# Three sub-layer boundaries of a two-layer decoder trunk, worked on 512 tokens at once instead of in two halves

## The chip, the core and the metric

The kernel runs on one core of a Trainium2 chip. That core has a matrix engine (TensorE, "PE" in the profile), an elementwise engine (VectorE, "DVE"), an activation engine (ScalarE, "ACT"), a general engine (GpSimd, "POOL") and DMA queues, most of them issued by SyncE ("SP"). Each engine executes its own instructions in the order in which the program wrote them, and waits for others by semaphores. On-chip operands lie in SBUF; matmul results lie in PSUM. The metric is the device time of one execution in microseconds (us), as the median of several runs.

## The reference

Two layers, one sequence of 512 tokens, 1024 features, FFN width 2816. Layer 0 mixes tokens by stick-breaking attention, layer 1 by sparse attention that an indexer selects. Each mixer, and each gated MLP behind it, gets a normed, scaled and shifted input, and its result is gated onto x:

```python
for i in range(DEPTH):
    mod = cond @ ada_w[i] + ada_b[i]
    sh1, sc1, g1, sh2, sc2, g2 = split(mod, 6)
    h = rms_norm(x, norm_mix[i]) * (1.0 + sc1) + sh1
    x = x + g1 * mixer_i(h)          # h @ w_in, attention, @ w_out
    h = rms_norm(x, norm_ffn[i]) * (1.0 + sc2) + sh2
    x = x + g2 * conv_ffn(h)         # u = h @ w_up; width-3 causal conv; silu(gate) * val; @ w_down

def rms_norm(x, g):                  # y = x / sqrt(mean(x*x) + 1e-6) * g
def dsa_attention(h, w_in, ...):     # proj = h @ w_in: 16 queries of 128, a latent of 128,
                                     # 8 indexer queries of 64, one indexer key of 64, 8 weights
```

So with s = gain * (1 + scale), a projection behind a norm is W^T (x * s * r) + W^T shift, where r is one number per token.

## The kernel before

Activations lie with features on the partitions and tokens along the row: x is eight tiles `x0` to `x7` of 128 features x 512 tokens. Every number that PE multiplies is split into a high part in a reduced format (fp32r) and the remainder, and each product is three matmuls (`mm3`, L250 to L252): high by high, low weight by high, high weight by low. A weight chunk of 128x1024 (512 KB) is loaded by DMA into one of six buffers of the pool `raws`, ACT copies its high part (`split_hi`, L210, tile `whi`), and DVE, or in the layer-1 attention sometimes POOL, subtracts for the low part (`split_lo`, L218, tile `wlo`). There are four `whi` and four `wlo` buffers. `order` lists the chunks in the order of their use; `fetch` loads ahead along it, and `chunk(key)` hands out a finished pair.

Nothing reorders the program: on each engine the instructions stand in the order in which the Python code issues them.

A **boundary** is the stretch from the last output projection of one sub-layer to the first projections of the next. There are three: 1 from layer 0's attention to its MLP, 2 from that MLP to layer 1's attention, 3 from that attention to layer 1's MLP (the start of the kernel and the last projection, `final_proj`, are written apart). In each, `last` names the four chunks of the output projection (eight result tiles `pt_l` of 128 features, each a sum over four 128-deep steps of three matmuls) and `first` the first four chunks of the next sub-layer: two pairs of gate and value columns of the MLP's up projection, or, in boundary 2, `kw` (indexer key and weights) and three query chunks. Their results are `pt_first`, eight steps of three matmuls each.

Before, a boundary goes through the tokens in two halves of 256 columns:

- half 0: per tile, the output projection, the update of x (`add_to_x`, L372 and DVE), ACT's square (`sqt`, five buffers), and the sum of the squares over tiles on DVE (`sqa`, L295);
- half 1 likewise, and among it the norm of half 0: the sum over features by a matmul with `ones_mean` (`pt_norm`, L300), ACT's reciprocal root as a seed (tile `ln`), one Newton step in three DVE instructions (`norm_newton`, L334 to L336), then per tile `u = r * sfac * x` on DVE (L343), the high part `hhi` with the shift on ACT, and the low part `hlo` on DVE (L352). The squares of half 1 are summed by PE itself in quarters (`quarter_squares`, tile `pt_part`, L307);
- the first two chunks on half 0, with the norm of half 1 among them, then the other two on half 0;
- `second_half`: the four chunks on half 1, each with what its `finish` does to the result. In the MLPs that is the evacuation `evac_up` with the width-3 convolution (tile `y`: one ACT and two DVE instructions, L998 to L1000), and after each second tile `mix` (L1017 a product, then the split into `acthi` and `actlo`, L234 and L235). In boundary 2 it copies the indexer keys `kd`, `kl` and queries; the indexer's scores `z` follow.

Matmuls in the boundaries therefore have 256 columns, elsewhere 512. `ada_dot` (L259) computes the modulation vectors `mod` on DVE from streamed chunks; it runs all through layer 0.

Of the kernel before, what the change touches and what calls it, by code (L numbers as in the profile page):

```python
# [18 lines left out]
D = 1024  # L19
# [40 lines left out]
def chunk_order():  # L60
    keys = []
    for l in range(DEPTH):
        for g in range(6):
            keys += [("ada", l, g, k) for k in range(KT)]
    for p in range(PAIRS):
        keys += [("q", p), ("k", p)]
    for g in range(4):
        keys += [("v", g, h) for h in range(2)]
    for nm in ("o", "do"):
        for g in range(2):  # L70
            keys += [(nm, g, m) for m in range(4)]
# [8 lines left out]
    keys += [("uv",)]  # L80
    return {k: i for i, k in enumerate(keys)}
# [38 lines left out]
def kernel_body(ctx, tc, xT, wst, cst, smalls, crow, ccol, relb, onehot, outT):  # L120
# [30 lines left out]
    sfac = cpool.tile([P, KT], F32, name="sfac")  # L151

# [132 lines left out]
    def square(f, hf):  # L285
        t = npool.tile([P, H2], F32, name="sqt", bufs=5)
        act.activation(t, x[f][:, halves[hf]], AF.Square)
        return t

    def square_add(f, t):  # L290
        if f == 0:
            a = sqs["acc"] = npool.tile([P, H2], F32, name="sqa")
# [4 lines left out]
    def sum_squares(t, start, stop):  # L297
        if start:
            sqs["pt"] = ptile([P, H2], "pt_norm", "z")
        pe.matmul(sqs["pt"], lhsT=ones_mean, rhs=t, start=start, stop=stop)  # L300

    def quarter_squares(ts, first):

        if first:
            sqs["parts"] = ptile([P, H2], "pt_part", "z")
        for i, t in enumerate(ts):
            pe.matmul(sqs["parts"][32 * i:32 * i + 32], lhsT=ones_mean[:, :32], rhs=t, start=first, stop=not first)  # L307

    def quarters_out():
        t = sqs["sum"] = npool.tile([P, H2], F32, name="sqt", bufs=5)  # L310
        act.activation(t, sqs["parts"], AF.Copy, scale=D / 32)
# [14 lines left out]
    def norm_seed(hf):  # L326
        ln = rstd[hf] = npool.tile([P, H2], F32, name="ln", bufs=2)
        act.activation(ln, sqs["pt"], AF.Abs_reciprocal_sqrt, bias=eps_c)
        rstd[hf, "ms"] = sqs["pt"]

    def norm_newton(hf):
        ln, ms = rstd[hf], rstd[hf, "ms"]
        t = npool.tile([P, H2], F32, name="nt")
        dve.tensor_mul(t, ln, ln)  # L334
        dve.scalar_tensor_tensor(t, ms, EPS, t, op0=OP.add, op1=OP.mult)
        dve.scalar_tensor_tensor(ln, t, 3.0, ln, op0=OP.subtract, op1=OP.mult)  # L336
# [3 lines left out]
    def norm_u(hf, f):  # L340
        c = halves[hf]
        u = us[hf, f] = npool.tile([P, H2], F32, name="u", bufs=4)
        dve.scalar_tensor_tensor(u, rstd[hf], sfac[:, f:f + 1], x[f][:, c], op0=OP.mult, op1=OP.mult)  # L343

    def norm_hi(l, sh, hf, f):
        act.activation(hcur["h"][f][0][:, halves[hf]], us[hf, f], AF.Identity,
                       bias=mod[l][:, sh * KT + f:sh * KT + f + 1])

    def norm_lo(l, sh, hf, f):
        c = halves[hf]  # L350
        hi, lo = hcur["h"][f]
        dve.scalar_tensor_tensor(lo[:, c], us.pop((hf, f)), mod[l][:, sh * KT + f:sh * KT + f + 1],  # L352
                                 hi[:, c].bitcast(F32), op0=OP.add, op1=OP.subtract)

    def norm_ops(l, sh, hf):

        for f in range(KT + 2):
            if f < KT:
                norm_u(hf, f)
                norm_hi(l, sh, hf, f)  # L360
            if f >= 2:
                norm_lo(l, sh, hf, f - 2)
            yield
# [25 lines left out]
    def boundary(last, O, l, gate, nxt, first):  # L389
# [3 lines left out]
        unsplit = lambda: pos["i"] <= order.index(last[3])  # L393
# [3 lines left out]
        fetch(pos["i"] + 1)  # L397

        begun = {}

        def out_steps(hf, m, ks):
            c = halves[hf]
            whi, wlo = cks[m // 2]
            if m not in begun:
                begun[m] = ptile([P, H2], "pt_l", "tr" if hf or m % 2 == 0 else "z")
            for k in ks:
                w = k * 256 + (m % 2) * P
                mm3(begun[m], whi[:, w:w + P], wlo[:, w:w + P], O[k][0][:, c], O[k][1][:, c], k == 0, k == 3)

        def out_tile(hf, m):  # L410

            if hf or m > 1:
                out_steps(hf, m, range(4))
            elif m == 0:
                for ks in (range(3), range(3, 4)):
                    for i in range(2):
                        out_steps(hf, i, ks)
            add_to_x(l, gate, m, begun.pop(m), halves[hf])
            return square(m, hf)

        prev = None
        for m in range(KT):
            t = out_tile(0, m)
            if prev is not None:
                square_add(m - 1, prev)
            prev = t
            if m in (0, 2) and unsplit():
                split_hi()
            if m in (1, 3):
                split_lo()  # L430
                if m == 3:
                    while unsplit():
                        split_hi()
                        split_lo()
# [4 lines left out]
        ops0 = norm_ops(nl, sh, 0)  # L439
        pend = []  # L440
        for m in range(KT):
            if m == 1:
                sum_squares(sqs["acc"], True, False)
                sum_squares(prev, False, True)
                norm_seed(0)
            if m == 5:
                quarter_squares(pend[:4], True)
            pend.append(out_tile(1, m))
            if m == 1:
                norm_newton(0)  # L450
            if m in (2, 4):
                split_hi()
            if m in (3, 5):
                split_lo()
            for _ in range((0, 0, 1, 1, 2, 1, 2, 2)[m]):
                next(ops0, None)
        for _ in ops0:
            pass
# [50 lines left out]
    def stick_layer(l):  # L509
        with ExitStack() as st:  # L510
# [445 lines left out]
            for i in range(HN):  # L956
# [16 lines left out]
                if i % 2:  # L973
# [6 lines left out]
            first = boundary([("o", 1, m) for m in range(4)], [O[4 + k] for k in range(4)], l, 2,  # L980
                             (l, S_NF, 3, 4), up_first(l))
# [5 lines left out]
    def ffn_layer(l, first, man):  # L987
        with ExitStack() as st:
# [43 lines left out]

            ys = []

            def finish(i, pt):
                ys.append(evac_up(i // 2, i % 2, pt))
                if i == 0:
                    warm(AF.Silu)
                if i % 2:
                    mix(i // 2, *ys[-2:])  # L1040

            second_half(first, finish)
# [13 lines left out]
            if l < DEPTH - 1:  # L1056
                return boundary(last, O, l, 5, (l + 1, S_NM, 0, 1),
                                [("kw",), ("qi", 0), ("qi", 1), ("qi", 2)]), man
# [3 lines left out]
    def dsa_layer(l, first, man):  # L1062
        with ExitStack() as st:
# [92 lines left out]
            with ExitStack() as si:  # L1156
# [18 lines left out]
                def finish(i, pt):  # L1175
                    if i:
                        if i < 3:
                            qi_evac(i - 1, pt)
                        return
                    act.activation(kd[:64], pt[:64], AF.Copy)  # L1180
                    act.activation(kd[64:], pt[:64], AF.Copy)
                    dve.tensor_sub(kl[:64], pt[:64], kd[:64].bitcast(F32))
                    dve.tensor_sub(kl[64:], pt[:64], kd[64:].bitcast(F32))
                    act.activation(kw, pt, AF.Copy)
# [5 lines left out]
                second_half(first, finish, (0, 2))  # L1190
# [54 lines left out]
                for h in range(IDX_HEADS):  # L1245
# [12 lines left out]
                    if h == 0:  # L1258
                        qi_evac(2, first[1][3])
# [442 lines left out]
```

## Time and profile before

| | us |
|---|---|
| time, median of 3 runs | 1281.17 (1280.67 to 1281.25) |
| the profiled execution's span | 1279.4 |
| PE busy in it | 1266.1 (99%) |
| DVE busy | 910.9 (71%) |
| ACT busy | 601.5 (47%) |
| POOL busy | 123.6 (10%) |
| PE's longest single wait | 1.0 |

The profiled execution has no time of its own beside its span; the span is 1.8 us under the median of the runs. PE is the engine to watch: it is busy in 99% of the span. DVE's and ACT's shares are averages over stages, and in a boundary an engine with a mean of 71% may well be the one that is late. POOL works almost only in layer 1's attention: 20 low parts of weight chunks (2397 ns each) and masks.

### The profile page before, as it was taken

What the parts mean: (1) busy time and instruction counts of PE and PEld (TensorE: products, weight loads), DVE (VectorE), ACT (ScalarE), POOL (GpSimd) and SP (SyncE); (2) the same over time, 40 slices, a digit from 0 to 9 for tenths busy, and PEclk for the clock granted to TensorE, in tenths of its full rate; (3) what the DMA queues carried; (4) which work ended last, traced back from release to release, by engine and by line L of the source; (5) the groups of instructions that cost most, each with busy time, mean ns of one, the idle gap of its engine ahead of it and who ended that gap; (6) DMA issues with size and microseconds to landing.
All of it is one profiled execution on the core that took longest, in us unless ns stands there. A gap on an engine that the chain in (4) does not pass through costs nothing.

```text
span 1279.4 us, 18069 instructions
## 1 busy us (share of the span) xinstructions
PE 1266.1 (99%) x6910; PEld 1055.4 (82%) x6910; DVE 910.9 (71%) x1551; ACT 601.5 (47%) x1067; POOL 123.6 (10%) x127
## 2 busy tenths in 40 slices
PE   8999999999999999999999999999999999999999
PEld 6888787898888888888997788778988888888888
DVE  5888998877777877886678876667866456456653
ACT  5476666455333423343455357775544334334430
POOL 0000000000000000000001457773000000000000
PEclk9999999999999999999999999999999999999999
DMA  9644443423575575654221311142221322423221
GB/s 375 215 132 132 132 131 117 148 67 101 195 250 189 179 238 201 194 183 151 88 78 67 99 50 50 50 144 71 83 90 68 124 95 74 127 83 98 75 91 66
DMA packets 50614, 163.23 MB, mean 128 GB/s; under 512 B 5808, under 2 KB 8624, under 8 KB 50528
## 3 DMA queue, kind: packets, MB, share of 16 engines
q1 hardware_dynamic: 50096, 161.30, 38.7%
q8 instruction: 54, 0.88, 0.3%
q10 hardware_dynamic: 432, 0.79, 0.2%
q14 instruction: 32, 0.26, 0.1%
HBM read 159.92 MB, written 2.14 MB: 127 GB/s over the span
## 4 chain that ended last, share of the span: by engine, by line
PE 91%; DVE 4%; ACT 1%; DMA 1%; issue 1%; POOL 1%; SPq 0%; ACTq 0%; DVEq 0%
PE pt_u L250 11%; PE pt_u L251 11%; PE pt_u L252 11%; PE pt_d L251 5%; PE pt_d L252 5%; PE pt_d L250 5%; PE pt_first L250 2%; PE pt_first L251 2%; PE pt_first L252 2%; PE pt_q L250 2%; PE pt_q L252 2%; PE pt_q L251 2%; PE pt_qk L250 2%; PE pt_l L251 2%; PE pt_l L252 2%; PE pt_l L250 2%
## 5 line engine op out<-in xcount | busy, mean ns | idle before, releaser
L210 ACT ACTIVATE whi<-raw 128x1024 fp32r<-128x1024 f32 (+1 forms) x206 | 205.2, 1002 | 117.7 <-PE pt_d L252 89.5
L250 PE MATMUL pt_u<-hhi,whi 128*128 128x512 f32 x640 | 249.2, 389 | 0.0
L251 PE MATMUL pt_u<-hhi,wlo 128*128 128x512 f32 x640 | 249.0, 389 | 0.0
L252 PE MATMUL pt_u<-hlo,whi 128*128 128x512 f32 x640 | 249.0, 389 | 0.0
L218 DVE TENSOR_TENSOR wlo<-raw,whi 128x1024 fp32r<-128x1024 f32 (+1 forms) x186 | 213.9, 1151 | 14.4 <-ACT whi L210 13.5
L998 ACT ACTIVATE y<-pt_u,sm 128x512 f32<-128x512 f32 x80 | 62.2, 777 | 188.4 <-PE pt_u L252 188.4
L250 PEld LDWEIGHTS pt_u<-hhi,whi 128*128 128x128 f32 x640 | 120.1, 188 | 26.1 <-issue 1.1
L251 PEld LDWEIGHTS pt_u<-hhi,wlo 128*128 128x128 f32 x640 | 120.1, 188 | 24.8
L252 PEld LDWEIGHTS pt_u<-hlo,whi 128*128 128x128 f32 x640 | 120.1, 188 | 24.8
L999 DVE SCALAR_TENSOR_TENSOR y<-pt_u,sm,y 128x511 f32<-128x511 f32 x80 | 59.9, 748 | 97.2 <-ACT y L998 97.0
L250 PE MATMUL pt_d<-acthi,whi 128*128 128x512 f32 x288 | 112.0, 389 | 0.0
L251 PE MATMUL pt_d<-acthi,wlo 128*128 128x512 f32 x288 | 112.0, 389 | 0.0
L252 PE MATMUL pt_d<-actlo,whi 128*128 128x512 f32 x288 | 112.0, 389 | 0.0
L259 DVE SCALAR_TENSOR_TENSOR raw<-raw,cond 128x1024 f32<-128x1024 f32 x88 | 106.5, 1216 | 3.7 <-DMA raw<-wst 3.7
L372 DVE SCALAR_TENSOR_TENSOR x<-pt_d,mod,x 128x512 f32<-128x512 f32 x48 | 36.0, 749 | 72.9 <-PE pt_d L252 72.9
L234 ACT ACTIVATE acthi<-y 128x512 fp32r<-128x512 f32 x44 | 27.8, 632 | 105.3 <-DVE y L1017 105.3
L250 PE MATMUL pt_first<-hhi,whi 128*128 128x256 f32 (+1 forms) x224 | 68.3, 305 | 0.2 <-ACT whi L210 0.2
L251 PE MATMUL pt_first<-hhi,wlo 128*128 128x256 f32 (+1 forms) x224 | 67.1, 300 | 0.9 <-DVE wlo L218 0.8
L252 PE MATMUL pt_first<-hlo,whi 128*128 128x256 f32 (+1 forms) x224 | 66.9, 299 | 0.0
L250 PEld LDWEIGHTS pt_d<-acthi,whi 128*128 128x128 f32 x288 | 54.1, 188 | 11.3
L251 PEld LDWEIGHTS pt_d<-acthi,wlo 128*128 128x128 f32 x288 | 54.1, 188 | 11.2
L252 PEld LDWEIGHTS pt_d<-actlo,whi 128*128 128x128 f32 x288 | 54.1, 188 | 11.1
(256 smaller groups left out, 2704.4 us busy)
## 6 DMA issues: line engine op xcount, KB each, us to landing
raw<-wst SPq DMA_DIRECT2D x250, 512.0 KB, 3.7
raw<-wst SPq DMA_DIRECT2D x48, 384.0 KB, 3.0
th<-rb SPq DMA_DIRECT2D x16, 256.0 KB, 3.4
ada<-wst SPq DMA_DIRECT2D x4, 512.0 KB, 6.2
outT<-x SPq DMA_DIRECT2D x16, 128.0 KB, 1.7
x<-xT SPq DMA_DIRECT2D x5, 256.0 KB, 5.0
x<-xT ACTq DMA_DIRECT2D x3, 256.0 KB, 3.9
cond<-crow SPq DMA_DIRECT2D x1, 512.0 KB, 10.5
```

Source lines behind the costliest of these rows:

```text
L210: act.activation(hi[:, :n], raw[:, :n], AF.Copy)
L218: engine.tensor_sub(lo[:, :n], raw[:, :n], hi[:, :n].bitcast(F32))
L234: act.activation(hi, src, AF.Copy)
L250: pe.matmul(out, lhsT=whi, rhs=ahi, start=start, stop=False)
L251: pe.matmul(out, lhsT=wlo, rhs=ahi, start=False, stop=False)
L252: pe.matmul(out, lhsT=whi, rhs=alo, start=False, stop=stop)
L259: dve.scalar_tensor_tensor(raw, raw, 1.0, cond, op0=OP.mult, op1=OP.mult, accum_out=dst)
L372: dve.scalar_tensor_tensor(x[f][:, c], pt, mod[l][:, g * KT + f:g * KT + f + 1], x[f][:, c], op0=OP.mult, op1=OP.add)
L998: act.activation(y, pt, AF.Identity, scale=cw[2], bias=sm[:, b + S_CB + c:b + S_CB + c + 1])
L999: dve.scalar_tensor_tensor(y[:, 1:], pt[:, :S - 1], cw[1], y[:, 1:], op0=OP.mult, op1=OP.add)
```

## The change

`boundary` now works on all 512 tokens. In order:

- per tile, output projection, update of x, ACT's square (two buffers of 512), DVE's sum. Beside these, the tile's scaled but unnormed value is split: ACT writes `x * sfac` as high part, DVE the low part (`scaled_lo`, L409). The pairs `xs` are put by `place` into buffers that are free at that time: `ohi`, `olo`, `kd`, `kz` in boundary 1, `acthi`, `actlo`, `y` in 2, `qh`, `ql` in 3;
- the first two chunks are projected from `xs`; after their second step PE takes one 512-wide sum of squares, and the seed and Newton step follow;
- then `u`, `hhi` and `hlo` as before, on 512 tokens, and step by step the other two chunks from these;
- the results of the first two chunks are multiplied by r (`rescale`, L355, DVE, tile `v`) and get W^T shift by ACT (`add_shift`, a bias column of `bcol`). The columns of `bcol` come from `shift_begin` (the shift goes out to DRAM and back as a row on all partitions, and the two chunks are loaded once more, transposed, as `bt`: three transfers into `raws` buffers) and `shift_dots` (two DVE instructions of 128x1024, L350). In boundaries 1 and 3 the loads are issued at the boundary's start and the dots stand behind the two `rescale`; for boundary 2 both lie earlier, inside the third down round of layer 0's MLP;
- `quarter_squares`, `quarters_out` and `second_half` are gone. All evacuations of the four first chunks stand together behind the boundary; in boundary 2 they are in `begin_scores`, where the low part `kl` of the second 64 partitions is now a copy on ACT;
- the low parts of weight chunks inside a boundary are computed on DVE in the first three tiles and on POOL from then on: 18 more POOL instructions in all, 38 for 20.

Two buffers outside change shape: `uvc` is two tiles of 512 instead of four of 256, and `vals` one copy of 512 instead of two of 256.

```diff
-    def boundary(last, O, l, gate, nxt, first):
+    def boundary(n, last, O, l, gate, nxt, first, place, shift=None):
...
+        late = shift is None
+        if late:
+            shift = shift_begin(n, nl, sh)
+        begun, xs, sq = {}, {}, {}
+        goals = {0: last[2], 1: last[3], 2: first[0], 4: first[1], 6: first[2]}
...
+        def scaled_lo(m):
+            hi, lo = xs[m]
+            dve.scalar_tensor_tensor(lo, x[m], sfac[:, m:m + 1], hi.bitcast(F32), op0=OP.mult, op1=OP.subtract)
+
+        for m in range(KT):
...
+            add_to_x(l, gate, m, begun.pop(m))
+            sq[m] = square(m)
+            xs[m] = place(m)
+            act.activation(xs[m][0], x[m], AF.Copy, scale=sfac[:, m:m + 1])
+            if m:
+                square_add(m - 1, sq.pop(m - 1))
+                if m == KT - 1:
+                    square_add(m, sq.pop(m))
+                scaled_lo(m - 1)
+            split_lo(engine=dve if m < 3 else pool)
+            if m in goals:
+                while pos["i"] <= order.index(goals[m]):
+                    split_hi()
...
+        scaled_lo(KT - 1)
+        split_lo(engine=pool)
...
+        split_hi()
+        split_lo(engine=pool)
+        hs = hcur["h"]
+
+        def first_steps(ids, src, k):
+            w = slice(k * P, (k + 1) * P)
+            for i in ids:
+                mm3(pts[i], cs[i][0][:, w], cs[i][1][:, w], src[k][0], src[k][1], k == 0, k == KT - 1)
+
+        for k in range(KT):
+            first_steps((0, 1), xs, k)
+            if k == 1:
+                sum_squares()
+                norm_seed()
+                norm_newton()
+        cs += [chunk(k, 0) for k in first[2:]]
+        for k in range(KT + 1):
+            if k < KT:
+                norm_hi(nl, sh, k)
+            if k == 5:
+                split_hi()
+                split_lo(engine=pool)
+            if k:
+                norm_lo(nl, sh, k - 1)
+                first_steps((2, 3), hs, k - 1)
+        split_hi()
+        split_lo(engine=pool)
+        return pts, shift if late else None
...
+    def shift_dots(shift):
+        n, row, ws = shift
+        for i, w in enumerate(ws):
+            dve.scalar_tensor_tensor(w, w, 1.0, row, op0=OP.mult, op1=OP.mult, accum_out=bcol[:, 2 * n + i:2 * n + i + 1])
+
+    def rescale(pt, new):
+        v = new()
+        dve.tensor_mul(v, pt, rstd["r"])
+        return v
+
+    def add_shift(n, i, v, out=None):
+        act.activation(v if out is None else out, v, AF.Identity, bias=bcol[:, 2 * n + i:2 * n + i + 1])
...
             def down(r):
                 j0, j1 = DOWN_ROUNDS[r]
                 for m in range(KT):
+                    if l == 0 and r == 2:
+                        if m == 1:
+                            early.append(shift_begin(1, 1, 0))
+                        if m == 5:
+                            shift_dots(early[0])
...
+            pts, shift = first
+            warm(AF.Silu)
+            vs = [rescale(pts[i], lambda: fp.tile([P, S], F32, name="v", bufs=2)) for i in range(2)]
+            if shift:
+                shift_dots(shift)
             ys = []
...
-            second_half(first, finish)
+            for i in range(4):
+                if i < 2:
+                    add_shift(2 * l, i, vs[i])
+                ys.append(evac_up(i // 2, i % 2, vs[i] if i < 2 else pts[i]))
                 if i % 2:
                     mix(i // 2, *ys[-2:])
```

How the order moves on two engines. First DVE in boundary 1, at the end of the output projection, as it stood before (`x_94` and so on are x's tiles, `sqa` the sum of squares, `nt` and `ln` the Newton step's):

```order
L295 TENSOR_TENSOR sqa<-sqa,sqt 128x256
L372 SCALAR_TENSOR_TENSOR x_98<-pt_l,mod_89,x_98 128x256
L295 TENSOR_TENSOR sqa<-sqa,sqt 128x256
L372 SCALAR_TENSOR_TENSOR x_99<-pt_l,mod_89,x_99 128x256
L295 TENSOR_TENSOR sqa<-sqa,sqt 128x256
L372 SCALAR_TENSOR_TENSOR x_92<-pt_l,mod_89,x_92 128x256
L372 SCALAR_TENSOR_TENSOR x_93<-pt_l,mod_89,x_93 128x256
L334 TENSOR_TENSOR nt<-ln 128x256
L335 SCALAR_TENSOR_TENSOR nt<-pt_norm,nt 128x256
L336 SCALAR_TENSOR_TENSOR ln<-nt,ln 128x256
```

And now, on DVE at the same place (`xkd`, `xkz` are the low parts of the scaled tiles):

```order
L297 TENSOR_TENSOR sqa<-sqa,sqt 128x512
L409 SCALAR_TENSOR_TENSOR xkd_2789<-x_98,sfac,xkd_2788 128x512
L368 SCALAR_TENSOR_TENSOR x_100<-pt_l,mod_89,x_100 128x512
L297 TENSOR_TENSOR sqa<-sqa,sqt 128x512 x2
L409 SCALAR_TENSOR_TENSOR xkz_2812<-x_99,sfac,xkz_2811 128x512
L409 SCALAR_TENSOR_TENSOR xkz_2837<-x_100,sfac,xkz_2836 128x512
L323 TENSOR_TENSOR nt<-ln 128x512
L324 SCALAR_TENSOR_TENSOR nt<-pt_norm,nt 128x512
L325 SCALAR_TENSOR_TENSOR ln<-nt,ln 128x512
L331 SCALAR_TENSOR_TENSOR u<-ln,sfac,x_93 128x512
```

The Newton step stood among the second half's updates of x; now it stands behind the last one, and behind all low parts of the scaled tiles.

Next DVE behind boundary 1, at the evacuation of the four first chunks, before:

```order
L1017 TENSOR_TENSOR y_3196<-y_3161,y_3196 128x512
L235 TENSOR_TENSOR actlo<-y_3196,acthi 128x512
L218 TENSOR_TENSOR wlo<-raw,whi 128x1024
L999 SCALAR_TENSOR_TENSOR y_3236<-pt_first,sm,y_3236 128x511
L1000 SCALAR_TENSOR_TENSOR y_3236<-pt_first,sm,y_3236 128x510
L218 TENSOR_TENSOR wlo<-raw,whi 128x1024
L999 SCALAR_TENSOR_TENSOR y_3266<-pt_first,sm,y_3266 128x511
L1000 SCALAR_TENSOR_TENSOR y_3266<-pt_first,sm,y_3266 128x510
L1017 TENSOR_TENSOR y_3266<-y_3236,y_3266 128x512
L235 TENSOR_TENSOR actlo<-y_3266,acthi 128x512
```

On DVE there now (`pt_u` are the results of the next up chunks):

```order
L997 TENSOR_TENSOR y_3020<-y_3015,y_3020 128x512
L237 TENSOR_TENSOR actlo<-y_3020,acthi 128x512
L979 SCALAR_TENSOR_TENSOR y_3030<-pt_first,sm,y_3030 128x511
L980 SCALAR_TENSOR_TENSOR y_3030<-pt_first,sm,y_3030 128x510
L979 SCALAR_TENSOR_TENSOR y_3034<-pt_first,sm,y_3034 128x511
L980 SCALAR_TENSOR_TENSOR y_3034<-pt_first,sm,y_3034 128x510
L997 TENSOR_TENSOR y_3034<-y_3030,y_3034 128x512
L237 TENSOR_TENSOR actlo<-y_3034,acthi 128x512
L220 TENSOR_TENSOR wlo<-raw,whi 128x1024
L979 SCALAR_TENSOR_TENSOR y_3075<-pt_u,sm,y_3075 128x511
```

The low parts that stood between the evacuations are gone from here (POOL computes them inside the boundary), but one: that of the first chunk of up(3), the pair after next, stands behind all four evacuations.

Last POOL, from the start of the kernel to the indexer's work tiles, before:

```order
L752 MEMSET kz_555 64x512
L1187 MEMSET work_6162 128x128
L1188 COPY work_6162<-cons 128x128
L1187 MEMSET work_6165 128x256
L1188 COPY work_6165<-cons 128x128
L1187 MEMSET work_6168 128x384
L1188 COPY work_6168<-cons 128x128
```

And now on POOL:

```order
L724 MEMSET kz_556 64x512
L220 ISA
L220 TENSOR_TENSOR wlo<-raw,whi 128x1024 x12
L1182 MEMSET work_5800 128x128
L1183 COPY work_5800<-cons 128x128
L1182 MEMSET work_5803 128x256
L1183 COPY work_5803<-cons 128x128
L1182 MEMSET work_5806 128x384
```

Boundaries 1 and 2 thus put twelve low parts on POOL, ahead of the indexer's work tiles.

More of the change, by code (lines that the diff above doesn't have):

```diff
@@ L283, in kernel_body, with square @@
     sqs = {}
-    def square(f, hf):
-        t = npool.tile([P, H2], F32, name="sqt", bufs=5)
-        act.activation(t, x[f][:, halves[hf]], AF.Square)
+    def square(f):
+        t = npool.tile([P, S], F32, name="sqt", bufs=2)
+        act.activation(t, x[f], AF.Square)
         return t
@@ L295, in square_add, with sum_squares @@
             dve.tensor_add(sqs["acc"], sqs["acc"], t)
[L297 to L311, printed above, removed]
+    def sum_squares():
+        sqs["pt"] = ptile([P, S], "pt_norm", "z")
+        pe.matmul(sqs["pt"], lhsT=ones_mean, rhs=sqs["acc"], start=True, stop=True)
     hcur = {}
@@ L345, in norm_hi @@
[L345 to L350, printed above, removed]
-        hi, lo = hcur["h"][f]
[L352 to L363, printed above, removed]
+    def norm_hi(l, sh, f):
+        u = us[f] = npool.tile([P, S], F32, name="u", bufs=3)
+        dve.scalar_tensor_tensor(u, rstd["r"], sfac[:, f:f + 1], x[f], op0=OP.mult, op1=OP.mult)
+        act.activation(hcur["h"][f][0], u, AF.Identity, bias=mod[l][:, sh * KT + f:sh * KT + f + 1])
@@ new lines, in norm_lo, with shift_begin @@
+    def norm_lo(l, sh, f):
+        hi, lo = hcur["h"][f]
+        dve.scalar_tensor_tensor(lo, us.pop(f), mod[l][:, sh * KT + f:sh * KT + f + 1],
+                                 hi.bitcast(F32), op0=OP.add, op1=OP.subtract)
+    def shift_begin(n, l, sh):
+        d = dp.tile([P, KT], F32, name=f"shd{n}")
+        nc.sync.dma_start(d, mod[l][:, sh * KT:(sh + 1) * KT])
+        row, ov = raws.tile([P, D], F32, name="shrow", tag="raw"), d[0:1, 0:1]
+        nc.sync.dma_start(row, bass.AP(tensor=ov.tensor, offset=ov.offset, ap=[[0, P], [1, D]]))
+        return n, row, [chunk_raw(("bt", n, i)) for i in range(2)]
@@ L415, in out_tile @@
+        for m in range(KT):
+            if m == 0:
                 for ks in (range(3), range(3, 4)):
                     for i in range(2):
[L417 to L434, printed above, removed]
+                        out_steps(i, ks)
+            elif m > 1:
+                out_steps(m, range(4))
+            add_to_x(l, gate, m, begun.pop(m))
[11 more added lines that the diff above has]
+                    split_hi()
@@ L1056, in ffn_layer, with place @@
             if l < DEPTH - 1:
-                return boundary(last, O, l, 5, (l + 1, S_NM, 0, 1),
-                                [("kw",), ("qi", 0), ("qi", 1), ("qi", 2)]), man
+                def place(f):
+                    if f < 7:
+                        return [fp.tile([P, S], F32R, name="x" + t, tag=t, bufs=11) for t in ("acthi", "actlo")]
+                    return [fp.tile([P, S], F32R, name=f"x{t}", tag=t) for t in ("y0", "y1")]
+                return boundary(1, last, O, l, 5, (l + 1, S_NM, 0, 1),
+                                [("kw",), ("qi", 0), ("qi", 1), ("qi", 2)], place, early[0]), man
             final_proj(last, O, l, 5)
@@ L1583, in dsa_layer, with place @@
                         follow(engine)
[L1584 removed]
+                def place(f):
+                    return [pp.tile([P, S], F32R, name="x" + t, tag=t, bufs=QRING) for t in ("qh", "ql")]
+                first = boundary(2, [("do", 1, m) for m in range(4)], O[4:], l, 2, (l, S_NF, 3, 4), up_first(l), place)
         return first, man
```

150 lines of the change are left out of this document (50 added, 100 removed).

## The prediction

> **What bounds the kernel now.** I read the page's first two parts, then what TensorE (PE) waited for, then PE in order of time across the three boundaries.
>
> ```profile
> PE 1266.1 (99%) x6910; PEld 1055.4 (82%) x6910; DVE 910.9 (71%) x1551; ACT 601.5 (47%) x1067; POOL 123.6 (10%) x127
> PEclk9999999999999999999999999999999999999999
> ...
> PE pt_part L307 <- ACT sqt L287: 3.0, 3, 1.0
> PE z L1406 <- DVE nm L1416: 2.0, 5, 0.7
> ```
>
> PE is never idle for long, and its clock is full everywhere. Its longest wait of all is 1.0 us, once in each boundary, for the squares of the second half. So a boundary is worth what PE's own work in it takes, plus what PE is made to wait. In order of time (start, duration):
>
> ```profile
> 245.71 0.39 PE L250 MATMUL pt_l<-ohi,whi 128*128 128x256 f32 x1
> ...
> 250.13 0.28 PE L250 MATMUL pt_l<-ohi,whi 128*128 128x256 f32 x1
> ...
> 258.65 0.28 PE L252 MATMUL pt_l<-olo,whi 128*128 128x256 f32 x1
> 258.77 0.60 PE L300 MATMUL pt_norm<-sqa,ones_mean 128*128 128x256 f32 x2
> 259.20 0.59 PE L300 MATMUL pt_norm<-sqt,ones_mean 128*128 128x256 f32 x2
> 259.44 0.47 PE L250 MATMUL pt_l<-ohi,whi 128*128 128x256 f32 x1
> 259.75 0.28 PE L251 MATMUL pt_l<-ohi,wlo 128*128 128x256 f32 x1
> ...
> 296.34 0.40 PE L250 MATMUL pt_u<-hhi,whi 128*128 128x512 f32 x1
> ...
> 613.61 0.28 PE L250 MATMUL pt_l<-acthi,whi 128*128 128x256 f32 x1
> ...
> 664.56 0.60 PE L1239 MATMUL pt_w<-cons,kw 128*128 128x128 f32 x4
> 664.91 0.36 PE L1251 MATMUL z<-kd,qs 128*128 128x256 f32 x1
> ...
> 886.57 0.28 PE L250 MATMUL pt_l<-ohi,whi 128*128 128x256 f32 x1
> ...
> 937.44 0.40 PE L250 MATMUL pt_u<-hhi,whi 128*128 128x512 f32 x1
> ...
> 1000.03 0.39 PE L250 MATMUL pt_d<-acthi,whi 128*128 128x512 f32 x1
> ...
> 1003.43 0.39 PE L250 MATMUL pt_d<-acthi,whi 128*128 128x512 f32 x1
> ```
>
> The three boundaries (1: layer 0's attention to its MLP; 2: that MLP to the sparse attention; 3: that to the last MLP) last 50.63, 50.95 and 50.87 us, from the first pt_l matmul to the first matmul behind. Between 250.13 and 258.65 lie 71 steps of a 256-wide matmul: 0.120 us each. Between 1000.03 and 1003.43 lie 15 steps of a 512-wide one: 0.2267. Two 256-wide sums of squares cost 1.10 (258.65 to 259.75) less two ordinary steps: 0.86.
>
> **PE's own work, a gain.** Before, 384 matmuls of 256 columns per boundary; now 192 of 512: 192 x 0.2267 = 43.5 us. Half sums and quarter sums (two, eight and one, with their wait) become one 512-wide sum over as many columns as the two above: 0.86, an estimate. Together 44.4 us, so 6.2, 6.6 and 6.5 us less: 19.3 in all, if PE never waits.
>
> **The chain that must keep up.** VectorE (DVE) now handles whole rows, and ACT and POOL feed it. Its steps, and the other engines':
>
> ```profile
> 295.82 0.69 DVE L235 TENSOR_TENSOR actlo<-y,acthi 128x512 fp32r<-128x512 f32 x1 [0.70 <-ACT acthi L234]
> 296.43 1.22 DVE L218 TENSOR_TENSOR wlo<-raw,whi 128x1024 fp32r<-128x1024 f32 x1
> 297.56 0.74 DVE L999 SCALAR_TENSOR_TENSOR y<-pt_first,sm,y 128x511 f32<-128x511 f32 x1
> 298.34 0.75 DVE L1000 SCALAR_TENSOR_TENSOR y<-pt_first,sm,y 128x510 f32<-128x510 f32 x1
> 299.01 1.21 DVE L218 TENSOR_TENSOR wlo<-raw,whi 128x1024 fp32r<-128x1024 f32 x1
> ...
> L259 DVE SCALAR_TENSOR_TENSOR raw<-raw,cond 128x1024 f32<-128x1024 f32 x88 | 106.5, 1216 | 3.7 <-DMA raw<-wst 3.7
> ...
> L210 ACT ACTIVATE whi<-raw 128x1024 fp32r<-128x1024 f32 x158 | 166.1, 1052 | 69.1 <-PE pt_d L252 55.6 <-PE pt_first L252 8.1 <-DMA raw<-wst 4.4
> L234 ACT ACTIVATE acthi<-y 128x512 fp32r<-128x512 f32 x44 | 27.8, 632 | 105.3 <-DVE y L1017 105.3
> ...
> L218 POOL TENSOR_TENSOR wlo<-raw,whi 128x1024 fp32r<-128x1024 f32 x20 | 47.9, 2397 | 96.5 <-ACT whi L210 96.4
> ```
>
> Back to back, DVE's steps come at 0.61 (two-operand, 512 wide), 0.67 (scalar and tensor; 0.78 where one needs the one before), 1.13 (a chunk's low part) and 1.2 (a dot). ACT takes 0.63 per 512, 1.05 per chunk; a POOL split 2.40.
>
> Take boundary 1, with zero at its first pt_l matmul. PE alone: projection to 21.8, two steps of the first chunks to 24.5, sum to 25.3, first two chunks to 33.5, next two to 44.4, up(2) (48 matmuls, 10.9) to 55.3. Before, up(3) began at 50.6 + 10.9 = 61.5. DVE, first without POOL: last pt_l result 21.9, x 22.7, ACT's square 23.4, last addition 24.1; sum ready 25.5, seed 26.2, three Newton steps 28.5, sixteen u and hlo (0.67 each, 0.72 of ACT ahead of the first) 40.3, two rescales 41, two shift dots 43.4, then eight y steps, two products, two low parts with ACT between, and the low part of up(3)'s first chunk: 55.3. That is the moment at which PE needs it. DVE has no slack, so what delays DVE delays PE.
>
> **What delays DVE.** Six chunks per boundary are now split on POOL. What such a split does to DVE shows where the two met before (DVE's rows, then POOL's):
>
> ```profile
> 881.11 2.52 DVE L1490 TENSOR_TENSOR olo<-bs,ohi 128x512 fp32r<-128x512 f32 x1
> ...
> 885.32 0.69 DVE L1490 TENSOR_TENSOR olo<-bs,ohi 128x512 fp32r<-128x512 f32 x1 [0.70 <-ACT ohi L1486]
> 885.93 1.59 DVE L372 SCALAR_TENSOR_TENSOR x<-pt_o,mod,x 128x512 f32<-128x512 f32 x2
> 887.44 1.30 DVE L320 SCALAR_TENSOR_TENSOR sfac<-mod,sm 128x8 f32<-128x8 f32 x1
> ...
> 880.72 2.36 POOL L218 TENSOR_TENSOR wlo<-raw,whi 128x1024 fp32r<-128x1024 f32 x1 [7.50 <-ACT whi L210]
> 886.32 2.40 POOL L218 TENSOR_TENSOR wlo<-raw,whi 128x1024 fp32r<-128x1024 f32 x1 [3.23 <-ACT whi L210]
> ```
>
> An olo that takes 0.69 alone took 2.52 and ended 0.55 behind POOL's split. An eight-column sfac took 1.30, to the split's end (888.72). The two x updates of 885.93, which read one operand from PSUM, went on beside the split. So I let a split stop every DVE step with two SBUF operands: square additions, xlo, u, hlo, dots, y from v, products; x updates and rescales pass. [...] Did splits stop nothing, the sum would be rival 1's.
>
> The splits, by ACT's order: (1) 11.3 to 13.7 and (2) 18.0 to 20.4 hit square additions; there are two square buffers, so ACT falls behind, and the last x ends at 23.6. (3) 24.1 to 26.5 falls between the last two additions: the sum starts at 27.1, PE waits 2.6. (4) 26.9 to 29.3 is half covered by DVE's wait for the seed, but holds the last two xlo: Newton is 1.6 later still. (5) 41.6 to 44.0, inside u and hlo: 2.3, PE waits 1.0 at the seventh step. (6) 46.4 to 48.8: rescales pass, the dots wait 1.2. Up(3)'s low part comes at 55.3 + 7.8 = 63.1, against 61.5: +1.6, PE waiting 4.0 there.
>
> Boundary 3 is the same with two more chunk splits on DVE early; its sum starts at 27.8: 63.8 against 50.9 + 10.9: +2.1. In boundary 2 PE reaches the transposes at 48.8, but the first z needs the first query block's low part: kv 47.5, then ACT's kw, two kd, kl, shifted qv and two query halves (at most L234's 0.63 each, kl's DVE part behind split 6) 52.4, and 0.69 on DVE: 53.1, against 664.91 - 613.61 = 51.3: +1.8.
>
> Sum +5.5. PE restarts add to each wait:
>
> ```profile
> 675.45 0.40 PE L252 MATMUL pt_lat<-hlo,whi 128*128 128x512 f32 x1
> 676.03 0.50 PE L1251 MATMUL z<-kd,qs 128*128 128x512 f32 x1 [0.18 <-ACT rl L1255]
> 676.36 0.39 PE L1252 MATMUL z<-kl,qs 128*128 128x512 f32 x1
> 676.60 0.39 PE L250 MATMUL pt_lat<-hhi,whi 128*128 128x512 f32 x1
> ```
>
> 1.15 us for three steps of 0.23, with 0.18 idle: some 0.2 beyond the idle, times nine waits, 1.7. Total about +7: 1279.4 of the profiled span becomes 1286.5, and the median of the runs, 1.8 above that span, 1288.
>
> At nothing I cost the shift's three DMAs per boundary:
>
> ```profile
> q1 hardware_dynamic: 50096, 161.30, 38.7%
> raw<-wst SPq DMA_DIRECT2D x250, 512.0 KB, 3.7
> ```
>
> The queue has room, and they are needed 40 us later; but they hold three of six raw buffers, and a chunk that waits for one would cost PE its 3.7 us of landing. At nothing, too, the two dots inside down round 2 (DVE has 0.75 + 0.95 of work per 4.1 us tile there), and in the attention one 512-wide vals copy for two of 256.
>
> **Rivals.** (1) POOL does not stop DVE. Then up(3) starts at 55.3 in boundaries 1 and 3 and z at 45.4: 6.2 + 6.4 + 5.9 = 18.5 less, 1262.7. For it: the x updates passed. Against it: both stretched rows. A half-way case, where fewer steps stop, lies between. (2) The chain is shorter than I add up, or the splits fall into its gaps: it has some sixty dependent steps, and 0.04 us on each moves a boundary by 2.4; three boundaries end at no change, 1281. (3) A long PE wait slows what follows. No row shows one: the longest is 1.0 us, the clock full. If after each of the three waits of 4 us the array did half its work for a further 15 matmuls' time (3.4 us), each costs 1.7: 1293. [...]
>
> **How the numbers follow.** A measurement tells about 0.2% (2.6 us) from no change. The forecast, 1284 to 1292: 0.42. Rival 3 and a chain longer than worked out: 0.12. Rival 2: 0.17. Rival 1 and half-way: 0.29. Hence slower 0.54, same 0.17, faster 0.29. The likeliest is 1288, its own range 1282 to 1294 (0.04 us per step to either side). The range of 8 in 10 reaches from 1264, which takes in the half-way cases but not all of rival 1, to 1297.
>
> **What would show it.** In the changed profile PE waits some 2.6 us for sqa at pt_norm three times, about 1 for hlo, and about 4 for wlo at the fifth pt_u tile or for qs at the first z. DVE's 512-wide u, hlo or additions have a longest duration near 3 us against 0.75. If instead no DVE step is longer than 0.8 and PE waits under 1 us, rival 1 holds. I am wrong in another way if PE waits on a DMA or on raw buffers, or if granted clock falls below 1.

## The result, and the profile after

The changed kernel takes 1291.93 us (median of 4 runs, 1289.81 to 1293.58), the kernel before 1281.21 (1280.67 to 1281.37): ratio 1.0083, 95% interval 1.0069 to 1.0098. It is slower by 10.7 us. The profiled execution has a span of 1290.2 us, against 1279.4 before: 10.8 more. The forecast was 1288, with a range of 1264 to 1297.

First the page's totals and clock, then the longest of what PE waited for (in all, times, longest):

```profile
PE 1261.8 (98%) x6274; PEld 1026.7 (80%) x6274; DVE 944.7 (73%) x1496; ACT 609.9 (47%) x1035; POOL 173.2 (13%) x145
PEclk9999999999999999999989999999999999999999
...
PE pt_norm L301 <- DVE sqa L297: 8.5, 3, 3.3
PE pt_u L252 <- ACT whi L212: 4.4, 2, 2.9
PE z L1246 <- DVE qs L1166: 3.0, 1, 3.0
...
PE pt_u L253 <- DVE wlo L220: 1.5, 2, 0.8
```

PE is busy for 4.3 us less than before, though its clock is no longer full everywhere. It waits 17.4 us for these four, where in the boundaries it had waited 3.0, for pt_part.

Where the 10.8 us lie is read from marks that both programs have: the first pt_l of each boundary and a matmul some way behind it (duration as minimum, median and maximum, then first and last start). The changed kernel:

```profile
245.69 0.50 PE L252 MATMUL pt_l<-ohi,whi 128*128 128x512 f32 x1
...
L174 PE MATMUL pt_b<-oh,rel x4: 427/433/438, 321.2 to 333.2; 32*16 32x320 f32 x4
L252 PE MATMUL pt_l<-acthi,whi x13: 389/389/389, 616.6 to 624.7; 128*128 128x512 f32 x13
L1212 PE MATMUL pt_kT<-cons,kn x4: 328/330/332, 707.5 to 708.3; 128*128 128x128 f32 x4
L252 PE MATMUL pt_l<-ohi,whi x9: 389/389/389, 894.2 to 899.6; 128*128 128x512 f32 x9
L252 PE MATMUL pt_d<-acthi,whi x11: 389/389/389, 1002.5 to 1009.3; 128*128 128x512 f32 x11
```

and the marks of the kernel before that were not shown yet:

```profile
L172 PE MATMUL pt_b<-oh,rel x4: 428/433/438, 318.2 to 330.2; 32*16 32x320 f32 x4
L1217 PE MATMUL pt_kT<-cons,kn x4: 328/328/329, 699.9 to 700.7; 128*128 128x128 f32 x4
L250 PE MATMUL pt_d<-acthi,whi x27: 389/389/389, 991.9 to 1009.5; 128*128 128x512 f32 x27
```

Boundary 1 to pt_b took 72.5 and takes 75.5; boundary 2 to pt_kT 86.3 and 90.9; boundary 3 to pt_d 105.3 and 108.3: 3.0, 4.6 and 3.0 us more. All of the loss is there.

Two things happen in each boundary. First, a POOL split stops DVE (POOL's rows, then DVE's rows in boundary 1; `v` is `rescale`, which reads PSUM; `cols` is a 128x1 step in boundary 2; the last row counts all of POOL's splits, with minimum, median and maximum):

```profile
257.57 2.41 POOL L220 TENSOR_TENSOR wlo<-raw,whi 128x1024 fp32r<-128x1024 f32 x1 [254.24 <-ACT whi L212]
...
287.41 6.59 POOL L220 TENSOR_TENSOR wlo<-raw,whi 128x1024 fp32r<-128x1024 f32 x2 [12.01 <-ACT whi L212]
...
257.86 2.67 DVE L297 TENSOR_TENSOR sqa<-sqa,sqt 128x512 f32<-128x512 f32 x1
...
288.19 3.56 DVE L336 SCALAR_TENSOR_TENSOR hlo<-u,mod,hhi 128x512 fp32r<-128x512 f32 x2
291.67 1.27 DVE L355 TENSOR_TENSOR v<-pt_first,ln 128x512 f32<-128x512 f32 x2
292.87 2.22 DVE L350 SCALAR_TENSOR_TENSOR raw<-raw,shrow 128x1024 f32<-128x1024 f32 x1
...
662.92 2.35 DVE L1065 SCALAR_TENSOR_TENSOR cols<-sm 128x1 f32<-128x1 f32 x1
...
L220 POOL TENSOR_TENSOR wlo<-raw,whi x38: 2358/2404/3792, 257.6 to 940.0; 128x1024 fp32r<-128x1024 f32 x38
```

The addition of 0.68 took 2.67 and ended 0.55 behind POOL's split. Two hlo took 3.56 where one takes 0.74, a dot 2.22 where it takes 1.22. The two rescales, inside POOL's sixth split (the second of the row at 287.41), took 0.63 each.

Second, behind most of the long waits PE runs at half speed for a while (first PE's rows, then windows: start and end, length, busy time of PE, PEld, DVE, ACT and POOL with their instructions, PEclk, and DMA's share and GB/s):

```profile
273.22 1.13 PE L301 MATMUL pt_norm<-sqa,ones_mean 128*128 128x512 f32 x2 [2.06 <-DVE sqa L297]
...
307.41 0.49 PE L252 MATMUL pt_u<-hhi,whi 128*128 128x512 f32 x1 [2.92 <-ACT whi L212]
308.67 0.53 PE L253 MATMUL pt_u<-hhi,wlo 128*128 128x512 f32 x1 [0.77 <-DVE wlo L220]
...
644.50 2.08 PE L301 MATMUL pt_norm<-sqa,ones_mean 128*128 128x512 f32 x2 [3.28 <-DVE sqa L297]
...
670.90 0.58 PE L1246 MATMUL z<-kd,qs 128*128 128x256 f32 x1 [2.96 <-DVE qs L1166]
...
922.04 1.12 PE L301 MATMUL pt_norm<-sqa,ones_mean 128*128 128x512 f32 x2 [3.19 <-DVE sqa L297]
...
956.22 0.49 PE L252 MATMUL pt_u<-hhi,whi 128*128 128x512 f32 x1 [1.49 <-ACT whi L212]
957.48 0.77 PE L253 MATMUL pt_u<-hhi,wlo 128*128 128x512 f32 x1 [0.77 <-DVE wlo L220]
...
273.00:276.00 3.00, 2.78 (x10) 2.00 (x11) 3.00 (x3) 0.69 (x1) 2.39 (x1) 1.00 0.56 175
309.00:312.00 3.00, 3.00 (x9) 2.34 (x8) 2.96 (x5) 1.27 (x2) 0.00 (x0) 0.50 0.50 175
646.00:650.00 4.00, 4.00 (x10) 2.86 (x9) 3.90 (x6) 0.69 (x1) 0.64 (x1) 0.50 0.62 217
671.00:674.00 3.00, 3.00 (x9) 2.61 (x10) 2.36 (x5) 1.72 (x4) 0.00 (x0) 0.50 0.00 0
923.00:926.00 3.00, 3.00 (x9) 2.36 (x8) 3.00 (x3) 0.69 (x1) 1.21 (x1) 0.57 0.55 184
958.00:961.00 3.00, 3.00 (x8) 2.31 (x7) 2.93 (x5) 1.09 (x2) 0.00 (x0) 0.51 0.54 176
```

Behind the wait of 2.06 the clock was full. Behind the other five (2.92 + 0.77, 3.28, 2.96, 3.19 and 1.49 + 0.77) it was half: for 6.83 us from 643.51 on, for 3.41 us the other four times. The last section reads from the traces behind which waits it came.

### The profile page after: what moved, and what is told of

It reads as the page before. It is cut to its first block, busy times and chain, and to the rows that moved or that the text cites. A ratio compares the mean times of both kernels' runs of the same rounds, so it can differ in the third digit from the quotient of the medians.

```text
span 1290.2 us, 16770 instructions
## 1 busy us (share of the span) xinstructions
PE 1261.8 (98%) x6274; PEld 1026.7 (80%) x6274; DVE 944.7 (73%) x1496; ACT 609.9 (47%) x1035; POOL 173.2 (13%) x145
## 4 chain that ended last, share of the span: by engine, by line
PE 82%; DVE 10%; issue 3%; ACT 3%; DMA 1%; POOL 1%; SPq 0%; DVEq 0%; ACTq 0%
PE pt_u L253 11%; PE pt_u L252 11%; PE pt_u L254 11%; PE pt_d L252 5%; PE pt_d L253 5%; PE pt_d L254 5%; PE pt_q L252 2%; PE pt_q L254 2%; PE pt_q L253 2%; PE pt_qk L252 2%; PE pt_qk L254 2%; PE pt_qk L253 2%; PE av L889 1%; DVE sqa L297 1%; PE tr L867 1%
## 5 line engine op out<-in xcount | busy, mean ns | idle before, releaser
L220 DVE TENSOR_TENSOR wlo<-raw,whi 128x1024 fp32r<-128x1024 f32 (+1 forms) x168 | 192.0, 1144 | 11.5 <-ACT whi L212 10.6
L220 POOL TENSOR_TENSOR wlo<-raw,whi 128x1024 fp32r<-128x1024 f32 x38 | 97.6, 2575 | 736.9 <-ACT whi L212 401.9
L254 PEld LDWEIGHTS pt_d<-actlo,whi 128*128 128x128 f32 x288 | 54.1, 188 | 11.3
L980 DVE SCALAR_TENSOR_TENSOR y<-pt_u,sm,y 128x510 f32<-128x510 f32 x80 | 59.9, 749 | 2.8
L1411 DVE CUSTOM_DVE_ANT_0 L<-z,L,cols 128x128 f32<-128x128 f32 (+1 forms) x64 | 34.8, 547 | 31.4 <-PE tr L1426 19.8
```

The costliest lines, as they stand in the source:

```text
L220: engine.tensor_sub(lo[:, :n], raw[:, :n], hi[:, :n].bitcast(F32))
L254: pe.matmul(out, lhsT=whi, rhs=alo, start=False, stop=stop)
L980: dve.scalar_tensor_tensor(y[:, 2:], pt[:, :S - 2], cw[0], y[:, 2:], op0=OP.mult, op1=OP.add)
L1411: dve.tensor_tensor_reduce(L, z[:, :ns], L, rq[:, c:c + 1], -USED, op0=OP.add, op1=OP.min, accum_out=nm[:, j:j + 1])
```

## The experiments

All compared with the kernel before on the same chip; before measured 1281.44 us beside the first four and 1281.32 beside the last four. Theory A holds that DVE's chain, lengthened by POOL's splits, sets the end of each boundary, and that half speed comes on top.

**Low parts on DVE** (`e1_low_dve`).

```diff
-            split_lo(engine=dve if m < 3 else pool)
+            split_lo()
...
-        split_lo(engine=pool)
+        split_lo()
```

> The changed kernel with the boundary's six low parts on DVE instead of POOL. Theory A (DVE's chain sets the end of each boundary, and a POOL split stops DVE for about as long as it lasts): in boundary 1 DVE lost 2.0, 2.2, 1.8, 2.1, 2.1 and 1.0 us to the six splits, 11.2, and pays 6 x 1.13 = 6.8 instead, so 4.4 less per boundary; the up(3) matmul and the first z start about 4 us earlier, and the time falls from 1292 to about 1278 (1274 to 1284). No DVE step of 512 columns is longer than 0.8. Rival B (POOL takes work off DVE, and DVE's chain is simply long): each low part costs DVE 1.13 more, 6.8 per boundary, and the time rises to about 1312.

Measured: 1287.99 us, ratio 1.0052 (1.0037 to 1.0067). No addition is longer than 0.693 now (2.669 in the changed kernel), and the wait at pt_norm is gone:

```profile
PE pt_u L252 <- ACT whi L212: 5.6, 2, 2.8
...
L297 DVE TENSOR_TENSOR sqa<-sqa,sqt x21: 678/680/693, 254.8 to 913.7; 128x512 f32<-128x512 f32 x21
...
284.73 1.22 DVE L220 TENSOR_TENSOR wlo<-raw,whi 128x1024 fp32r<-128x1024 f32 x1 [1.74 <-ACT whi L212]
...
306.23 0.51 PE L252 MATMUL pt_u<-hhi,whi 128*128 128x512 f32 x1 [2.84 <-ACT whi L212]
```

Rival B is refuted, since nothing rose. But the gain is 4 us, not 14: up(3) started at 306.23 instead of 307.41. The stops during the output projection had lain partly beside DVE's own waits for pt_l, and a low part in DVE's order waited 1.74 us for ACT. In boundary 1 the sum of squares was ready 2.6 us earlier behind the boundary's start, but up(3) only 1.0. The size of theory A was wrong, and where the boundary's end is set stayed open.

**Low parts left out** (`e2_low_left_out`).

```diff
+    def skip_lo():
+        while pend_lo:
+            k, n, raw, hi = pend_lo.pop(0)
+            ready[k] = (hi, hi)
...
-            split_lo(engine=dve if m < 3 else pool)
+            split_lo() if m < 3 else skip_lo()
...
-        split_lo(engine=pool)
+        skip_lo()
```

> The changed kernel in which the six low parts per boundary are left out (the high part is used a second time as a weight, so the matmuls stay as many). Theory A: DVE's chain is 11.2 us shorter per boundary, PE becomes the bound again, up(3) starts at 55 to 56 us behind the boundary's start instead of 61.7, no long PE wait is left, and with it the half-speed stretches go: 7 + 1.6 less per boundary, time 1262 to 1269. Rival B: POOL's work is hidden already; only what waits for a low part changes, and the time stays at 1288 to 1293.

Measured: 1264.15 us, ratio 0.9868 (0.9851 to 0.9884), the clock 1.000 throughout. PE's longest wait in a boundary is the 0.3 at the first z. The marks:

```profile
L257 PE MATMUL pt_l<-ohi,whi x6: 392/395/499, 245.8 to 249.4; 128*128 128x512 f32 x6
L174 PE MATMUL pt_b<-oh,rel x4: 427/433/438, 313.1 to 325.1; 32*16 32x320 f32 x4
L257 PE MATMUL pt_l<-acthi,whi x25: 389/389/389, 608.5 to 624.8; 128*128 128x512 f32 x25
L1217 PE MATMUL pt_kT<-cons,kn x4: 328/330/332, 688.9 to 689.7; 128*128 128x128 f32 x4
```

Boundary 1 takes 67.3 to pt_b and boundary 2 80.4 to pt_kT: 5.2 and 5.9 less than before. So the wider matmuls are worth 17 us in all where DVE can follow. In this order of the work the low parts, with the stops, waits and half speed that come of them, cost 28 on POOL and, by the first experiment, 24 on DVE.

**Waits filled with matmuls** (`e3_fill_waits`).

```diff
+                    if j == 3 and which == 0:
+                        for _ in range(13):
+                            pe.matmul(pt, lhsT=hs[0][0][:, :P], rhs=hs[0][0], start=True, stop=True)
```

and the same ahead of the first z.

> The changed kernel with 13 more matmuls of 512 columns (2.95 us, results overwritten) ahead of the first matmul of up(3) in both MLPs and ahead of the first z. They fill waits of 2.9 + 0.8, 1.5 + 0.8 and 3.0 us. Theory A with the clock's gate as its second part (a PE wait of about 2.3 us or more is followed by some 3.2 us at a granted clock of 0.5, which costs 1.6): the waits go into the added matmuls, the half-speed stretch behind each goes, and the time falls by 3 to 5 us, to about 1288, the granted clock there being 1.0. Rival C (the half-speed stretch costs nothing, since DVE is the bound there too): no change within 1 us, 1292.

Measured: 1288.69 us, ratio 1.0055 (1.0040 to 1.0070), granted clock 0.997 instead of 0.992. More work on PE made the kernel 3.2 us faster, so half speed behind the last wait of a boundary costs time; rival C is refuted. Boundaries 1 and 3 became 1.7 and 1.4 shorter, boundary 2 only 0.7: there PE waited 2.1 us at pt_w, where the changed kernel has no such wait. The clock of 0.997 is worth two half-speed stretches of 3.41 us (an estimate: half of 6.8 us is 0.0027 of the span of 1286.9). One lies in boundary 3, where matmuls come 0.42 us apart instead of 0.23 from about 921.75 on; that the other lies behind this wait at pt_w is an estimate too, from the smaller gain there. The same profile shows that the length of a wait doesn't decide alone. Boundary 2's wait at pt_norm was as long as in the changed kernel, and behind it the clock stayed full:

```profile
643.42 1.12 PE L301 MATMUL pt_norm<-sqa,ones_mean 128*128 128x512 f32 x2 [3.27 <-DVE sqa L297]
643.98 0.79 PE L252 MATMUL pt_first<-xacthi,whi 128*128 128x512 f32 x1
644.62 0.39 PE L253 MATMUL pt_first<-xacthi,wlo 128*128 128x512 f32 x1
```

**Sum of squares later** (`e4_sum_later`).

```diff
-            if k == 1:
+            if k == 3:
                 sum_squares()
```

> The changed kernel with the sum of squares behind the fourth step of the first two chunks instead of the second (0.91 x 2 = 1.8... 2.7 us of PE work put ahead of it). The waits at pt_norm (2.1, 3.3, 3.2) all but vanish, and the half speed behind two of them. Theory A: DVE's chain ends where it ended, so PE waits at up(3) and at the first z for as much longer; the time stays within 2 us of 1292 (1289 to 1293). Rival D (these waits are on PE's path and simply add up): 8.5 of waits and 3.2 of half speed go, and the time falls to about 1280.

Measured: 1293.12 us, ratio 1.0089 (1.0074 to 1.0104). The waits moved, as theory A said:

```profile
PE pt_u L252 <- ACT whi L212: 7.0, 2, 3.5
PE z L1246 <- DVE qs L1166: 3.5, 1, 3.5
...
PE pt_w L1234 <- ACT kw L359: 2.4, 1, 2.4
...
PE pt_norm L301 <- DVE sqa L297: 1.2, 2, 0.6
```

The changed kernel's largest item of waiting, 8.5 us at pt_norm, was thus not what the time hung on: with 7.3 of it gone, PE waited at least as much longer at later places, and the time didn't fall.

**up(3) split earlier** (`e5_up3_early`), on top of the first experiment. The theory is now divided: is it the sum of DVE's work (A1), or only that up(3)'s split stands behind all evacuations on ACT and DVE (A2)?

```diff
                 shift_dots(shift)
+            split_hi()
+            split_lo()
             ys = []
...
+                if i == 2:
+                    split_hi()
+                    split_lo()
```

> The low parts on DVE as in e1_low_dve, and the two chunks of up(3) split earlier: high and low part of the first right behind the shift's dots, of the second behind the third evacuation, instead of behind all four evacuations. In e1_low_dve PE waited 2.8 + 0.8 us in boundary 1 and 2.8 + 0.5 in boundary 3 for them, each with a half-speed stretch (1.6) behind. Theory A2 (what ends the boundary is the place of up(3)'s split behind the evacuations in ACT's and DVE's order, not the sum of DVE's work): both waits and their half speed go, 5 us per boundary, time 1288 to about 1278. Theory A1 (DVE's whole work is the bound): the wait moves to up(4) or to a result buffer, and the time stays at 1286 to 1289.

Measured: 1277.79 us, ratio 0.9970 (0.9959 to 0.9981): 10.2 less than the first experiment, and below the kernel before. No instruction was taken away. Both waits for whi are gone; 0.7 us for result buffers (`y`), 0.4 for wlo, and the waits of boundary 2 and for hlo are left:

```profile
PE z L1251 <- DVE qs L1171: 3.5, 1, 3.5
PE pt_first L254 <- DVE hlo L336: 2.8, 3, 1.2
```

A1 is refuted: DVE may be late with the evacuations for a while, as long as nothing that PE needs next stands behind them.

**Three more edits of the order** (`e6_all_three`), on top of the fifth experiment.

```diff
             if k == 5:
                 split_hi()
-                split_lo()
             if k:
                 norm_lo(nl, sh, k - 1)
+                if k == 6:
+                    split_lo()
...
-        split_hi()
-        split_lo()
+        if late:
+            split_hi()
+            split_lo()
...
                 begin_scores()
+                split_hi()
+                split_lo()
...
+                drain(fill, 5)
                 ptw = ptile([P, S], "pt_w", "tr")
```

> e5_up3_early, and three more edits of order: the low part of the fifth split one step later (DVE waited 1.74 us there for ACT), in boundary 2 the last split behind the start of the scores, and five of the eight steps of the projection pt_qi, which the scores' loop used as filler, ahead of the transposes. Theory A2: boundary 2's waits (1.1 at pt_w, 3.5 at z, and half speed) shrink by 4 to 6, the hlo waits by 1 to 2.7; time 1270 to 1274, below the kernel before (1281). Theory A1: less work is nowhere done, so no more than 2 us below e5_up3_early.

Measured: 1269.76 us, ratio 0.9914 (0.9898 to 0.9931), the clock 1.000. This version beats both kernels, the changed one by 22 us. The largest item of waiting left in the boundaries is 2.5 us at the scores, for ACT's relu; at pt_norm it is 0.2. What each of the three edits gained was not measured singly.

```profile
PE z L1256 <- ACT rl L1260: 2.5, 4, 0.9
```

**No dots** (`e7_no_dots`).

```diff
+    dve.memset(bcol, 0.0)
...
-        n, row, ws = shift
-        for i, w in enumerate(ws):
-            dve.scalar_tensor_tensor(w, w, 1.0, row, op0=OP.mult, op1=OP.mult, accum_out=bcol[:, 2 * n + i:2 * n + i + 1])
+        pass
```

> The changed kernel without the shift's dots (the bias columns are zero, so the shift is left out of the first two chunks; the loads stay). Theory A: in boundaries 1 and 3 the two dots (1.2 each, and 1.0 more behind a POOL split in boundary 1) lie on DVE's chain to up(3): 2.4 to 3.4 us less in each, 5 to 7 in all, time 1285 to 1287. Rival B: DVE has room there, nothing changes: 1291 to 1293.

Measured: 1284.97 us, ratio 1.0028 (1.0017 to 1.0039): 7.0 under the changed kernel, the upper end of the expectation. The shift's dots lay on the path to up(3), whose wait for whi shrank from 2.9 to 0.2 us in boundary 1 and is gone in boundary 3.

**All three, with the low parts on POOL** (`e8_all_three_pool`). As the sixth kernel, with `engine=pool` where the changed kernel has it.

> e6_all_three with the boundary's six low parts on POOL again, as in the changed kernel. Theory A (a POOL split stops DVE for about its own length): the waits for the sum of squares (2.1, 3.3, 3.2) and half speed behind two of them come back, and DVE is up to 4.4 us later per boundary: 8 to 14 us above e6_all_three. Rival B2 (only the order of the work was wrong, POOL or DVE is all the same): within 2 us of e6_all_three.

Measured: 1281.09 us, ratio 0.9995 (0.9986 to 1.0004): 11.3 above the sixth kernel. The addition of squares stretches again, and PE waits for it:

```profile
PE pt_norm L301 <- DVE sqa L297: 8.5, 3, 3.3
...
L297 DVE TENSOR_TENSOR sqa<-sqa,sqt x21: 672/677/2668, 256.6 to 913.1; 128x512 f32<-128x512 f32 x21
```

In the mended order making the low parts on POOL costs 11 us; in the changed kernel, with up(3) behind everything, 4 us of it showed.

## Why the prediction was right, and where it was not

**PE's own work: right, a little too high.** 19.3 us less was forecast if PE never waits; with the low parts left out, where PE waits at most 0.3 in a boundary, 17.3 were measured.

**POOL's splits stop DVE: right,** in both directions. Steps with two SBUF operands stretched (an addition 2.67 us for 0.68, a dot 2.22 for 1.22), rescales passed (0.63 each). One step that the list doesn't name was stopped too: a 128x1 `cols` took 2.35 us in boundary 2, where it took 0.15 in the kernel before, as the sfac was stopped before (1.30). POOL can also be the one that waits: its fifth split, from 287.41, took 3.79 us, 1.4 more than the usual 2.40, while the DVE steps of 287.53 and 288.19 took 0.74 each, as ever. So the order in which the two begin doesn't decide alone: the addition of 257.86 began behind the split of 257.57 and was stopped, these two DVE steps began behind the split of 287.41 and passed it.

**The waits: two of three places right.** At pt_norm 2.6 was forecast, and 2.06, 3.28 and 3.19 measured. For up(3) 63.1 us behind the boundary's start was forecast; its second matmul, the first that needs the low part, started at 308.67 - 245.69 = 63.0. (It lies in the third `pt_u` tile, not in the fifth as the prediction counts.) For the first z 53.1 was forecast: 670.90 - 616.6 = 54.3. The wait of 1.0 for hlo didn't come: the fifth split began when seven of the eight u were done (287.41), not amid them.

**What set up(3): the chain right, its reading too strong.** The prediction put the start down to DVE's low part, and that did come last, 0.77 us behind ACT's high part. But PE waited the first 2.92 us for the high part, which stands behind `acthi` of the second mix; ACT and DVE alternate there and are late together. What fails is "DVE has no slack, so what delays DVE delays PE": the fifth experiment only moved the splits of up(3) and gained 10.2 us over the first, with no less work on DVE.

**The sum of 5.5: right in total, not place by place.** For 1.6 in boundary 1, 1.8 in boundary 2 and 2.1 in boundary 3 the runs show 1.2, 3.0 and 1.3: the second matmul of up(3) starts 63.0 and 63.3 behind the start of boundaries 1 and 3, and started 61.8 and 62.0 behind it before (first two rows below, kernel before); the first z starts 54.3 behind that of boundary 2, and started 51.3 behind it. That these errors cancel to 5.5 is luck.

```profile
307.47 0.39 PE L251 MATMUL pt_u<-hhi,wlo 128*128 128x512 f32 x1
...
948.57 0.39 PE L251 MATMUL pt_u<-hhi,wlo 128*128 128x512 f32 x1
```

**Half speed: left out of the forecast.** It was rival 3, with 1.7 for each of three waits, and a share of 0.12; and a granted clock below 1 was a sign of being wrong that the prediction named. It came, behind five of six waits, three of them at the end of a boundary, where nothing covers it. Beyond the 5.5 the marks show 1.8, 1.6 and 1.7 in boundaries 1 to 3, and the half-speed rows account for it: in boundary 1, nine steps of up(3) from 308.67 on took 3.74 us where nine take 2.04. So 5.5 for lateness and 5.1 for half speed make the 10.6 at the marks. The forecast had 1.7 for PE's restarts in that place, an estimate that no run shows by itself (the row it is taken from has 0.29 beyond the idle time, not 0.2). Filling the waits got 3.2 of the 5.1 back. Rival 3's time, 1293, was nearer than the forecast's 1288. Its 3.4 us at half work were a supposition that no row of the kernel before shows; the trace of the changed kernel shows 3.41 us at a clock of 0.50 four times and 6.83 once. The length of a wait alone doesn't tell which one slows PE: 3.28 us was followed by half speed in one kernel, 3.27 in another was not. In the changed kernel's trace the half-speed stretches start whole multiples of 3.413 us apart, whatever work lies between, and PE's idle time within one such length tells the cases apart (last section). Runs of one kernel differ in the clock too: the sixth took 1268.6 us at a granted clock of 1.000 and 1272.27 at 0.996. The changed kernel's 1289.81 at 0.994 and 1293.58 at 0.991 fit, its 1291.89 at 0.989 is out of line.

**Costed at nothing: right.** PE waited for no weight chunk's DMA in a boundary, and boundary 2's early dots made no wait in the down round.

## What to carry to other kernels

When a stage is made cheaper for the engine that bounds it, look at the first thing that the next stage needs and at what stands ahead of it in every engine's order; here the splits of two weight chunks in each of two boundaries, moved ahead of evacuations that nobody waited for yet, decided 10 us. The largest wait in a profile need not cost anything: 8.5 us at pt_norm were free as long as a later wait ended last. With the later waits mended, the same 8.5 made most of the eighth kernel's 11. Low parts given to a second engine were not free here: compare the time for which a split on POOL stopped DVE (1.99 us at the addition that took 2.67 for 0.68, 1.00 at the dot that took 2.22 for 1.22) with what the low part would have cost DVE (1.13).

## What was not expected of the hardware

Behind a wait of about 3 us PE ran at half speed in most cases, but not in all: behind 2.06 it did not, behind 1.49 + 0.77 with one matmul between it did, behind 3.28 it did, behind 3.27 in another kernel it did not. The changed kernel's trace holds a record of the granted clock, and it tells the cases apart there. Every half-speed stretch in its boundaries lasts 3.41 or 6.83 us, and their starts lie whole multiples of 3.413 us apart: they are 309.01, 643.51, 670.82, 923.40 and 957.54, with 98, 8, 74 and 10 multiples between them. So in this trace the clock changes at the edges of windows of 3.413 us, and what goes with it is how long PE is idle inside one:

| wait | PE idle in the window (us) | clock in the next window |
|---|---|---|
| changed kernel, boundary 1, 2.06 at pt_norm | 1.76 | 1.00 |
| boundary 1, 2.92 + 0.77 at up(3) | 2.59 | 0.50 |
| boundary 2, 3.28 at pt_norm | 2.29 | 0.50 |
| boundary 2, 2.96 at the first z | 2.88 | 0.50 |
| boundary 3, 3.19 at pt_norm | 2.05 | 0.50 |
| boundary 3, 1.49 + 0.77 at up(3) | 2.26 | 0.50 |
| third experiment, boundary 2, 3.27 at pt_norm | about 1.7, then 1.6 | full (matmuls 0.23 us apart) |

The last row's edge is an estimate, reckoned back by 82 times 3.413 us from about 921.75, where that run's matmuls begin to come 0.42 us apart. In the changed kernel's trace, from 20 us after the start on, the clock was half behind each of the five full-speed windows with 2.05 us of idle time or more, and behind none of the 360 with 1.79 or less. In the kernel before none of 367 windows has more than 0.98, and the clock stays at 1.00. The half-speed window from 643.51 on, with 0.98 idle, was followed by another at half; the other five, with at most 0.08, by full speed. The wait of the last row, which by that estimate fell across the edge of two windows, had no half speed behind it. This is read from the traces, where the ends of matmuls are modelled; no experiment shifted a wait across an edge on purpose.

And added matmuls whose results are thrown away made the kernel 3.2 us faster (1288.69 against 1291.93).
